# Gate products of an encoder's feed-forward layers by seven quarter-block products, with half of the weight sums made by accumulating DMAs

## The chip, the cores and the metric

The kernel runs on one core of a Trainium2 chip. Its time is device microseconds of one execution, the median of three runs. TensorE (PE in the rows) multiplies, with a second row for its weight loads (PEld); VectorE (DVE), ScalarE (ACT) and GpSimd (POOL) work beside it; SyncE (SP) issues the loads from HBM.

## The reference, cut to what matters

Two layers of an encoder over 512 tokens and width 1024. Each layer is a feed-forward block, a mixer, and a second feed-forward block, so there are four feed-forward blocks (called block 0 to 3 here). Layer 0 mixes by two kinds of attention, layer 1 by convolutions.

```
def swiglu(x, w_gate, w_up, w_down):          # w_gate, w_up: 1024 x 2816
    return (jax.nn.silu(x @ w_gate) * (x @ w_up)) @ w_down
x = x + 0.5 * swiglu(rms_norm(x, ffn_norm[i, 0]), ...)
x = x + mixer(rms_norm(x, mix_norm[i]))
x = x + 0.5 * swiglu(rms_norm(x, ffn_norm[i, 1]), ...)
```

## The kernel before

**Numbers in two parts.** Activations lie as 8 tiles of 128 features x 512 tokens. Each float32 operand is split into a high part (ScalarE's cast, `split`, L146) and a low part (VectorE's subtraction, L147), and each product is three matmuls, high x high, high x low, low x high (`mm3`, L126 to L128).

**A feed-forward block.** The 2816 hidden features are 22 tiles (index f). A tile of `w_gate` or `w_up` is 128 partitions x 1024 columns, 512 KB: eight 128x128 weight blocks, one for each tile of the contraction. A plain product of one tile is 8 x 3 = 24 matmuls of 512 columns (`chunk`). A gate goes through SiLU (`gated`), is multiplied by the up product, and is split again (`hidden`). After 22 tiles the down product follows, 8 output tiles of 22 x 3 matmuls.

**Pairs.** For f = 4 to 19 two hidden tiles are taken together (`pair`). The gate products of the two are plain, 48 matmuls of 512 columns. The up products of both are one product of 2 x 2 blocks (two tiles by two halves of the contraction, times two halves of the contraction by two halves of the tokens) by seven quarter products in place of eight (a Strassen-Winograd scheme): 7 x 4 x 3 = 84 matmuls of 256 columns. Their left factors are sums of weight quarters (`sums`, four VectorE additions of 128x512), their right factors sums of activation quarters (`halves`, made once for each block in four steps, each of some ten small operations on VectorE and ScalarE). The seven results are put together by one ScalarE copy and seven VectorE additions of 128x256. The matmuls of the gates and of the quarter products alternate.

**Weights on their way.** `plan` lists the loads (units) and the splits (pieces of 128x512, each the weights of 12 matmuls); `piece` hands out a piece and sees to it that the next three are loaded, summed and split. Units go through three buffers (`raw`), the two up tiles of a pair through two more (`ux`); high and low pieces have five buffers each. All loads of weights are issued on SP's queue in order (L82), each when its buffer is free. The order of instructions on each engine is fixed when the program is built, by the scheduler of the framework; each engine goes through its list in order.

**Attention.** In the mixer of layer 0, 64 units of attention (32 of one kind, then 32 of the other) run as a pipeline of scores, softmax, transposes (L710) and products with the values. Projections stand between them as fillers: for each unit `mixer_ab` adds 1.6 (first 32 units) or 1.45 (after) blocks of three matmuls.

Of the kernel before, what the change touches and what calls it, by code (L numbers as in the profile page):

```python
# [9 lines left out]
F32 = mybir.dt.float32  # L10
# [13 lines left out]
PAIRS = (4, 20)  # L24
# [4 lines left out]
class Trunk:  # L29
    def __init__(self, ctx, tc, a, out):  # L30
# [8 lines left out]
        self.fr = pool("fr", 1)  # L39
# [19 lines left out]
    def plan(self, units):  # L59


        self.units, self.pieces = [], []
        for u in units:
            i = len(self.units)
            if len(u) == 4:
                g0, g1, u0, u1 = u
                self.units += [(g0, False), (u0, True), (u1, True), (g1, False)]
                A, B = slice(0, 512), slice(512, 1024)
                self.pieces += [(i, A), (i + 1, A), (i + 1, B), (i, B), (i + 2, 0), (i + 2, 1), (i + 3, A), (i + 2, 2), (i + 2, 3), (i + 3, B), (i + 2, B)]
                continue  # L70
            src, cut = u
            self.units.append((src, False))
            w = src.shape[1]
            self.pieces += [(i, slice(c, min(w, c + cut))) for c in range(0, w, cut)]
        self.loaded, self.ready, self.used = [], [], 0
        self.share, self.extra, self.extra_end, self.look = 0, None, 0, 3

    def load(self, upto):
        while len(self.loaded) < min(upto + 1, len(self.units)):
            src, held = self.units[len(self.loaded)]  # L80
            t = (self.ux if held else self.raw).tile([P, 1024], F32, tag="raw", name=self.name("raw"))
            self.nc.sync.dma_start(t[:, : src.shape[1]], src)  # L82
            self.loaded.append(t)

    def sums(self, i):
# [5 lines left out]
        s1, s2, s3, s4 = (self.t() for _ in range(4))  # L91
# [94 lines left out]
    def norm(self, after=None):  # L186

        nc = self.nc
        s = self.fr.tile([P, 2, T], F32R, tag="fr", name=self.name("ss"))
# [28 lines left out]
    def ffn(self, own, gain, natural=False, start=False):  # L218
# [4 lines left out]
        with self.tc.tile_pool(name=self.name("hp"), bufs=NF) as hp, self.tc.tile_pool(name=self.name("ux"), bufs=2) as self.ux, self.tc.tile_pool(name=self.name("tp"), bufs=4) as tp:  # L223
            hs, held = [], []
            if start:
# [13 lines left out]
                xs = list(self.xs)  # L239
            prep = self.halves(hp, tp, own)  # L240
            f = 2 if start else 0
            while f < NF:
                if PAIRS[0] <= f < PAIRS[1]:
                    self.go(prep)
                    hs += self.pair(hp, xs, fold)
# [4 lines left out]
                if f == 0:  # L250
# [8 lines left out]
                    self.norm(AF.Silu)  # L259
                else:  # L260
                    self.go(self.chunk(pg, xs))
                    if held:
                        self.norm(AF.Silu)
# [64 lines left out]
    def pair(self, hp, xs, fold):  # L328

# [3 lines left out]
        gates = [self.ps("g"), self.ps("g")]  # L333
        both = ((j, n) for j, ps in enumerate(gates) for n, _ in enumerate(self.chunk(ps, xs)))
        sn, uu, u0 = self.t(), self.t(), self.t()
        gate = []

        def blocks(n):
            for _ in range(n):
                j, k = next(both)  # L340
                if k == NK - 1:
                    gate.append(self.gated(gates[j], fold))

        def product(tag, x):
            ps = self.ps(tag, 256)
# [10 lines left out]
        blocks(2)  # L356
        q1 = product("g", b11)
        nc.scalar.copy(sn[:, L], q1)
        blocks(2)
        add(u0[:, L], product("d", b21), sn[:, L])  # L360
        blocks(2)
        add(sn[:, R], product("d", part(1)), sn[:, L])
        blocks(2)
        q5 = product("g", part(0))
        add(u0[:, R], q5, sn[:, R])
        blocks(2)
        add(uu[:, L], product("d", part(2)), sn[:, R])
        add(uu[:, R], q5, uu[:, L])
        blocks(2)
        add(u0[:, R], product("d", b22), u0[:, R])  # L370
        blocks(2)
        q4 = product("d", part(3))
        h0 = self.t()
        nc.vector.tensor_tensor(h0, u0, gate[0], op=ALU.mult)
        out = [self.hidden(hp, h0)]
        blocks(2)
        add(uu[:, L], q4, uu[:, L])
        h1 = self.t()
        nc.vector.tensor_tensor(h1, uu, gate[1], op=ALU.mult)
        return out + [self.hidden(hp, h1)]  # L380
# [204 lines left out]
    def put(self, t, p, half):  # L585
# [6 lines left out]
        if half == 1:  # L592
            f = self.t()[:, :n]
            if t % 2 == 0:
                nc.scalar.activation(f, p[:, :n], AF.Copy, scale=r)
            else:
                nc.vector.tensor_scalar(f, p[:, :n], r, 1.0, op0=ALU.mult, op1=ALU.mult)
            p, r = f, None
# [5 lines left out]
        for src, hi, lo in parts:  # L604
            if half == 1:
                nc.gpsimd.tensor_copy(hi, src)
                nc.vector.tensor_tensor(lo, src, hi.bitcast(F32), op=ALU.subtract)
                continue
# [186 lines left out]
    def mixer_ab(self, gain):  # L795
        nc = self.nc
        with ExitStack() as ctx:
            pool = lambda name, bufs: ctx.enter_context(self.tc.tile_pool(name=name, bufs=bufs))
            self.vp, self.up, self.ptp = pool("vp", 4), pool("up", 14), pool("ptp", 4)
# [20 lines left out]
            with self.tc.manual_schedule(engines={mybir.EngineType.PE}):  # L820
# [6 lines left out]
                for i in range(n + 5):  # L827
# [7 lines left out]
                    due += (1.6 if i < 32 else 1.45) / 2  # L835
# [3 lines left out]
                    due += (1.6 if i < 32 else 1.45) / 2  # L839
# [94 lines left out]
    def gated_pair(self, j):  # L934
        nc = self.nc
        pg, pa = self.ps("g"), self.ps("g")
        if j == 0:
# [7 lines left out]
            self.norm(AF.Sigmoid)  # L945
# [147 lines left out]
    def ffn_units(self, i):  # L1093
        a = self.a
        u = []
        for f in range(NF):
# [6 lines left out]
            elif PAIRS[0] <= f < PAIRS[1]:  # L1103
                if f % 2 == 0:
                    u.append((g, a["gate"][i, f + 1], v, a["up"][i, f + 1]))
# [117 lines left out]
```

## Time and profile before

| what | value |
|---|---|
| median of three runs | 1828.51 us (1827.61 to 1831.22) |
| the profiled execution | 1826.34 us, its span 1824.6 us |
| granted TensorE clock, mean | 0.996 |
| busy, share of the span | PE 99%, PEld 85%, DVE 68%, ACT 46%, POOL 10% |
| DMA | 181.79 MB, 31.1% of the 16 engines' time on SP's queue |

A row of a timeline has the start in us, the duration, the engine, the line of the kernel, the operation, its tiles, and in brackets how long the engine had been idle and what it had waited for. Durations of neighbours on one engine overlap, since they are pipelined: what an instruction takes of an engine in a dense stretch is the distance between starts. In the rows `psg`, `psd`, `psm` are the PSUM tiles of the three tags g (four buffers), d (two) and m (two).

### The profile page before, as it was taken

What the parts mean: (1) busy time and instruction counts of PE and PEld (TensorE: products, weight loads), DVE (VectorE), ACT (ScalarE), POOL (GpSimd) and SP (SyncE); (2) the same over time, 40 slices, a digit from 0 to 9 for tenths busy, and PEclk for the clock granted to TensorE, in tenths of its full rate; (3) what the DMA queues carried; (4) which work ended last, traced back from release to release, by engine and by line L of the source; (5) the groups of instructions that cost most, each with busy time, mean ns of one, the idle gap of its engine ahead of it and who ended that gap; (6) DMA issues with size and microseconds to landing.
All of it is one profiled execution on the core that took longest, in us unless ns stands there. A gap on an engine that the chain in (4) does not pass through costs nothing.

```text
span 1824.6 us, 25574 instructions
## 1 busy us (share of the span) xinstructions
PE 1805.4 (99%) x9532; PEld 1555.3 (85%) x9532; DVE 1240.1 (68%) x2211; ACT 842.7 (46%) x1536; POOL 187.2 (10%) x213
## 2 busy tenths in 40 slices
PE   9999999999999999999999999999999999999997
PEld 7899888889878899988888999888888889998886
DVE  6877734488987877764448777634499688887333
ACT  6544433357776544443335444433364554444332
POOL 0000000004432000000000000000389100000000
PEclk9999999999999999999999999999999999999999
DMA  5232233333243232333332332233322232323332
GB/s 198 81 105 93 93 96 95 98 103 99 68 132 114 94 103 96 102 113 96 96 101 81 101 108 93 89 95 96 126 93 93 81 105 94 103 99 96 92 100 66
DMA packets 57675, 181.79 MB, mean 100 GB/s; under 512 B 6352, under 2 KB 8656, under 8 KB 57552
## 3 DMA queue, kind: packets, MB, share of 16 engines
q1 hardware_dynamic: 56976, 179.33, 31.1%
q8 instruction: 75, 1.23, 0.3%
q10 hardware_dynamic: 576, 0.84, 0.1%
q14 instruction: 48, 0.39, 0.1%
HBM read 175.43 MB, written 2.10 MB: 97 GB/s over the span
## 4 chain that ended last, share of the span: by engine, by line
PE 94%; DVE 4%; ACT 1%; DMA 1%; issue 1%; DVEq 0%; SPq 0%; ACTq 0%
PE psg L127 16%; PE psg L126 16%; PE psg L128 16%; PE psd L127 15%; PE psd L128 15%; PE psd L126 15%; PE psm L710 1%; DVE pt L717 1%; DVE wl L147 0%; DMA bias<-in_bias 0%; PE psg L740 0%; PE psg L739 0%; DVE m L673 0%; DVE t L690 0%; PE psg L672 0%
## 5 line engine op out<-in xcount | busy, mean ns | idle before, releaser
L146 ACT CAST wh<-raw 128x512 fp32r<-128x512 f32 (+1 forms) x630 | 380.2, 606 | 616.4 <-PE psd L127 411.9
L147 DVE TENSOR_TENSOR wl<-raw,wh 128x512 fp32r<-128x512 f32 (+1 forms) x556 | 374.5, 674 | 303.3 <-ACT wh L146 297.8
L127 PE MATMUL psg<-xs,wh 128*128 128x512 f32 (+1 forms) x1200 | 455.6, 380 | 0.3 <-DVE xs L156 0.3
L126 PE MATMUL psg<-xs,wh 128*128 128x512 f32 (+1 forms) x1200 | 455.2, 380 | 0.6 <-ACT xs L155 0.6
L128 PE MATMUL psg<-xs,wl 128*128 128x512 f32 (+1 forms) x1200 | 453.2, 378 | 0.0
L128 PE MATMUL psd<-h,wl 128*128 128x512 f32 (+1 forms) x726 | 277.9, 383 | 0.0
L127 PE MATMUL psd<-h,wh 128*128 128x512 f32 (+1 forms) x726 | 277.9, 383 | 0.0
L126 PE MATMUL psd<-h,wh 128*128 128x512 f32 (+1 forms) x726 | 277.7, 383 | 0.0
L128 PEld LDWEIGHTS psg<-xs,wl 128*128 128x128 f32 x1200 | 225.9, 188 | 41.2
L126 PEld LDWEIGHTS psg<-xs,wh 128*128 128x128 f32 x1200 | 226.5, 189 | 37.4 <-ACT xs L155 1.2
L127 PEld LDWEIGHTS psg<-xs,wh 128*128 128x128 f32 x1200 | 226.5, 189 | 36.7 <-DVE xs L156 0.9
L147 POOL TENSOR_TENSOR wl<-raw,wh 128x512 fp32r<-128x512 f32 (+1 forms) x74 | 97.5, 1328 | 766.4 <-ACT wh L146 766.2
L126 PEld LDWEIGHTS psd<-h,wh 128*128 128x128 f32 x726 | 136.4, 188 | 26.8
L128 PEld LDWEIGHTS psd<-h,wl 128*128 128x128 f32 x726 | 136.4, 188 | 26.6
L127 PEld LDWEIGHTS psd<-h,wh 128*128 128x128 f32 x726 | 136.4, 188 | 26.4
L146 ACT CAST wh<-t 128x512 fp32r<-128x512 f32 x128 | 79.4, 621 | 88.2 <-PE psg L127 47.7
L355 DVE TENSOR_TENSOR t<-psd,t 128x256 f32<-128x256 f32 x160 | 67.8, 423 | 71.2 <-PE psd L128 71.2
L126 PE MATMUL psd<-tt,wh 128*128 128x256 f32 x384 | 108.5, 283 | 1.8 <-ACT wh L146 1.8
L128 PE MATMUL psd<-tt,wl 128*128 128x256 f32 x384 | 108.9, 284 | 0.1
L127 PE MATMUL psd<-tt,wh 128*128 128x256 f32 x384 | 108.7, 283 | 0.0
L126 PE MATMUL psd<-xs,wh 128*128 128x256 f32 (+1 forms) x344 | 108.1, 314 | 0.0
L128 PE MATMUL psd<-xs,wl 128*128 128x256 f32 (+1 forms) x344 | 106.9, 311 | 0.0
(275 smaller groups left out, 2702.6 us busy)
## 6 DMA issues: line engine op xcount, KB each, us to landing
raw<-in_up SPq DMA_DIRECT2D x83, 512.0 KB, 3.6
raw<-in_gate SPq DMA_DIRECT2D x83, 512.0 KB, 3.5
raw<-in_down SPq DMA_DIRECT2D x64, 448.0 KB, 3.3
raw<-in_down SPq DMA_DIRECT2D x32, 512.0 KB, 3.5
raw<-in_cdin SPq DMA_DIRECT2D x18, 512.0 KB, 3.5
raw<-in_abqk SPq DMA_DIRECT2D x13, 512.0 KB, 3.5
raw<-in_about SPq DMA_DIRECT2D x16, 256.0 KB, 2.7
bias<-in_bias SPq DMA_DIRECT2D x8, 512.0 KB, 3.5
```

The source lines that it names most:

```text
L126: mm(ps, lhsT=aH, rhs=bH, start=first, stop=False)
L127: mm(ps, lhsT=aH, rhs=bL, start=False, stop=False)
L128: mm(ps, lhsT=aL, rhs=bH, start=False, stop=last)
L146: self.nc.scalar.copy(hi, src)
L147: (eng or self.nc.vector).tensor_tensor(lo, src, hi.bitcast(F32), op=ALU.subtract)
L355: add = lambda to, a, b: nc.vector.tensor_tensor(to, a, b, op=ALU.add)
L710: nc.tensor.transpose(ps[:, i * P : (i + 1) * P], pr[:, i * P : (i + 1) * P], self.ident)
L717: nc.vector.tensor_tensor(lo, src, hi.bitcast(F32), op=ALU.subtract)
```

## The change

**Both products by seven.** In 18 pairs (`BOTH`: four, five, five and four in blocks 0 to 3) the gate products, too, are made by seven quarter products. `pair` now calls a generator `seven` once (other pairs) or twice (these pairs). The pairs named here as double pairs have 168 matmuls of 256 columns and none of 512; the 13 single pairs keep 48 and 84. Block 0 begins its pairs at f = 6, not 4, so there are 31 pairs and not 32, and of its four `halves` steps one now follows each of f = 2 to 5.

**Two of four sums by DMA.** The signs of the scheme are turned so that all four sums of weights are additions. Of these, VectorE makes two (L109, L110). The other two are made while loading: the first quarter of the second tile is loaded twice, into both halves of its buffer (L93, L94), and then GpSimd's queue adds the first tile's quarter into one half (L95) and the second tile's second quarter into the other (L96), by accumulating DMAs of 256 KB that wait for the plain loads. The second quarter by itself goes to a tile of its own (L97, `a22`). A summed unit has thus five DMAs of 256 KB in place of one of 512 KB.

**Smaller edits.** The last projection of the attention's values is scaled and split out of PSUM by ScalarE and VectorE at once (`put`), without the copy and GpSimd's casts. The fillers between units are paced at 1.6 to unit 31, 1.8 to unit 50, 1.35 after. One buffer (`fr`) moves to the mixer's pools.

```
-PAIRS = (4, 20)
+PAIRS = ((6, 20), (4, 20), (4, 20), (4, 20))
+BOTH = ((8, 10, 14, 16), (6, 8, 12, 14, 18), (6, 8, 12, 14, 18), (6, 10, 14, 18))
...
+            if held in (2, 4):
+                A, B = slice(0, 512), slice(512, 1024)
+                a22 = self.a22[len(self.loaded)] = self.ux.tile([P, 512], F32, tag="a22", name=self.name("a22"), bufs=2)
+                self.nc.sync.dma_start(t[:, A], src[:, A])
+                self.nc.sync.dma_start(t[:, B], src[:, A])
+                self.nc.gpsimd.dma_start(t[:, A], self.units[len(self.loaded) - 1][0][:, A], accum_op=ALU.add)
+                self.nc.gpsimd.dma_start(t[:, B], src[:, B], accum_op=ALU.add)
+                self.nc.sync.dma_start(a22, src[:, B])
...
-        nc.vector.tensor_tensor(s1, b[:, A], b[:, B], op=ALU.add)
-        nc.vector.tensor_tensor(s2, a[:, A], s1, op=ALU.subtract)
-        nc.vector.tensor_tensor(s3, b[:, A], a[:, A], op=ALU.subtract)
-        nc.vector.tensor_tensor(s4, a[:, B], s2, op=ALU.add)
-        self.sum4 = s2, s1, s3, s4
+        s2, s4 = self.t(), self.t()
+        nc.vector.tensor_tensor(s2, a[:, A], b[:, B], op=ALU.add)
+        nc.vector.tensor_tensor(s4, a[:, B], s2, op=ALU.add)
+        self.sum4 = s2, b[:, B], b[:, A], s4, self.a22[i]
...
+        if both:
+            for g in self.seven(xs, "gdggdgd", lambda: None):
+                nc.vector.tensor_tensor(g, g, self.rB, op=ALU.mult)
+                nc.scalar.activation(g, g, AF.Silu)
+                if not fold:
+                    nc.vector.tensor_tensor(g, g, self.rB, op=ALU.mult)
+                gate.append(g)
...
-                    next(prep, 0)
+                    if not start:
+                        next(prep, 0)
...
-                    due += (1.6 if i < 32 else 1.45) / 2
+                    due += (1.6 if i < 32 else 1.8 if i < 51 else 1.35) / 2
```

**What moves, in three places.** The first is VectorE in block 0, ahead of the first pair (f = 4): `x`, `par` and `tt` belong to `halves`, `raw` alone to the sums of weights (L92, L93), `wl` to low parts. Before:

```order
L317 TENSOR_TENSOR t_589<-x 128x256
L147 TENSOR_TENSOR tt_410<-t_472,tt_410 128x256
L322 SCALAR_TENSOR_TENSOR t_591<-x,par,t_590 128x256
L323 SCALAR_TENSOR_TENSOR t_530<-x,par,t_528 128x256
L92 TENSOR_TENSOR t_623<-raw_544 128x512
L147 TENSOR_TENSOR tt_525<-t_528,tt_525 128x256
L147 TENSOR_TENSOR tt_412<-t_474,tt_412 128x256
L321 SCALAR_TENSOR_TENSOR t_589<-t_589,par,t_590 128x256
L320 SCALAR_TENSOR_TENSOR tt_524<-t_589,par,tt_524 128x256
L147 TENSOR_TENSOR tt_526<-t_591,tt_526 128x256
L147 TENSOR_TENSOR tt_527<-t_530,tt_527 128x256
```

In the changed program, around the products of f = 4, which are plain now:

```order
L303 TENSOR_TENSOR t_634<-psg_564,rB_378 128x512
L162 TENSOR_TENSOR wl_619<-raw_582,wh_618 128x512
L162 TENSOR_TENSOR tt_452<-t_550,tt_452 128x256
L162 TENSOR_TENSOR wl_666<-raw_582,wh_665 128x512
L311 TENSOR_TENSOR t_638<-psg_565,t_635 128x512
L335 TENSOR_TENSOR t_647<-x 128x256
L162 TENSOR_TENSOR wl_684<-raw_616,wh_683 128x512
L340 SCALAR_TENSOR_TENSOR t_649<-x,par,t_648 128x256
L339 SCALAR_TENSOR_TENSOR t_647<-t_647,par,t_648 128x256
L162 TENSOR_TENSOR h_640<-t_638,h_640 128x512
L338 SCALAR_TENSOR_TENSOR tt_643<-t_647,par,tt_643 128x256
```

Where two steps of `halves` and the sums stood in one stretch, less than one step now stands among the gate (L303, L311) and the low parts of plain products.

The second is VectorE in block 1. Before, around the sums of the pair f = 6 (`h` is a hidden tile, L355 puts quarter products together, L285 takes a gate from PSUM):

```order
L92 TENSOR_TENSOR t_7115<-raw_7045 128x512
L93 TENSOR_TENSOR t_7116<-raw_6934,t_7115 128x512
L94 TENSOR_TENSOR t_7117<-raw_7045,raw_6934 128x512
L147 TENSOR_TENSOR h_7094<-t_7092,h_7094 128x512
L95 TENSOR_TENSOR t_7118<-raw_6934,t_7116 128x512
L147 TENSOR_TENSOR wl_7124<-t_7116,wh_7123 128x512
L147 TENSOR_TENSOR wl_7148<-t_7115,wh_7147 128x512
L355 TENSOR_TENSOR t_7101<-psd_7146,t_7099 128x256
L147 TENSOR_TENSOR wl_7167<-raw_7047,wh_7166 128x512
L147 TENSOR_TENSOR wl_7178<-t_7117,wh_7177 128x512
L285 TENSOR_TENSOR t_7200<-psg_7097,rB_6537 128x512
L147 TENSOR_TENSOR wl_7206<-t_7118,wh_7205 128x512
```

In the changed program, at the passage from the double pair f = 8 to the single pair f = 10. The last low part from the buffer that `raw_7816` takes over (that of `raw_7566`) stands four rows ahead of these; L365 and L366 put quarter products together, L402 multiplies by the gate:

```order
L162 TENSOR_TENSOR wl_7799<-a_1743_7567,wh_7798 128x512
L365 TENSOR_TENSOR t_7740<-psg_7779,t_7740 128x256
L162 TENSOR_TENSOR wl_7824<-raw_7674,wh_7823 128x512
L366 TENSOR_TENSOR t_7741<-t_7740,psg_7797 128x256
L162 TENSOR_TENSOR wl_7845<-raw_7715,wh_7844 128x512
L366 TENSOR_TENSOR t_7742<-t_7740,psd_7815 128x256
L162 TENSOR_TENSOR wl_7867<-raw_7715,wh_7866 128x512
L365 TENSOR_TENSOR t_7741<-psg_7841,t_7741 128x256
L366 TENSOR_TENSOR t_7742<-psg_7797,t_7742 128x256
L162 TENSOR_TENSOR wl_7893<-raw_7674,wh_7892 128x512
L402 TENSOR_TENSOR t_7741<-t_7741,t_7599 128x512
L109 TENSOR_TENSOR t_7905<-raw_7715,raw_7816 128x512
```

Four sums have become two, and evictions of quarter products (`psg`, `psd`, 128x256) stand between the low parts; the sum in the last row is the one that waits for an accumulating DMA (`raw_7816`).

The third is SP's queue in block 1, in the pairs f = 6 to 10. Before, one load for each tile:

```order
L82 DMA raw_7113<-in_gate 128x1024
L82 DMA raw_7045<-in_up 128x1024
L82 DMA raw_7277<-in_gate 128x1024
L82 DMA raw_7164<-in_up 128x1024
L82 DMA raw_7343<-in_gate 128x1024
```

In the changed program:

```order
L99 DMA raw_7674<-in_gate 128x1024
L97 DMA a_1713_7418<-in_gate 128x512
L99 DMA raw_7523<-in_up 128x1024
L93 DMA raw_7566<-in_up 128x512
L94 DMA raw_7566<-in_up 128x512
L97 DMA a_1743_7567<-in_up 128x512
L99 DMA raw_7842<-in_gate 128x1024
L99 DMA raw_7903<-in_gate 128x1024
L97 DMA a_1794_7817<-in_up 128x512
L99 DMA raw_7715<-in_up 128x1024
L93 DMA raw_7816<-in_up 128x512
```

A summed tile (`raw_7566`, `raw_7816`) has become two loads of half its size and a third for its own quarter (`a_1743_7567` is `a22`). The accumulating DMAs onto it stand on GpSimd's queue.

## Rows read from the trace of the kernel before

**Rows 1.** Engines on the page: busy time, share of the span, instructions.
```profile
PE 1805.4 (99%) x9532; PEld 1555.3 (85%) x9532; DVE 1240.1 (68%) x2211; ACT 842.7 (46%) x1536; POOL 187.2 (10%) x213
```
**Rows 2.** The chain that ended last, by engine: share of the span.
```profile
PE 94%; DVE 4%; ACT 1%; DMA 1%; issue 1%; DVEq 0%; SPq 0%; ACTq 0%
```
**Rows 3.** Windows: two pairs, then down product; length, busy (instructions), PEclk, DMA share, GB/s.
```profile
684.81:726.97 42.16, 42.16 (x266) 38.10 (x265) 32.68 (x57) 18.81 (x34) 0.00 (x0) 1.00 0.30 100
...
1200.00:1300.00 100.00, 100.00 (x443) 82.84 (x442) 41.51 (x65) 31.40 (x54) 0.00 (x0) 1.00 0.32 93
```
**Rows 4.** Timeline of ScalarE: the copy of one pair and of the pair two later.
```profile
684.81 0.37 ACT L358 COPY t<-psg 128x256 f32<-128x256 f32 x1
...
726.97 0.36 ACT L358 COPY t<-psg 128x256 f32<-128x256 f32 x1
```
**Rows 5.** Timeline of TensorE: first and last of 20 quarter matmuls, and the next.
```profile
668.81 0.28 PE L128 MATMUL psd<-tt,wl 128*128 128x256 f32 x1
...
671.08 0.28 PE L128 MATMUL psg<-tt,wl 128*128 128x256 f32 x1
671.20 0.40 PE L128 MATMUL psg<-xs,wl 128*128 128x512 f32 x1
```
**Rows 6.** Timeline of VectorE in a pair, back to back, then a sum that needs the one before.
```profile
685.32 0.68 DVE L95 TENSOR_TENSOR t<-raw,t 128x512 f32<-128x512 f32 x1
685.92 1.29 DVE L147 TENSOR_TENSOR wl<-t,wh 128x512 fp32r<-128x512 f32 x2
687.12 0.42 DVE L355 TENSOR_TENSOR t<-psd,t 128x256 f32<-128x256 f32 x1
687.46 0.68 DVE L147 TENSOR_TENSOR wl<-raw,wh 128x512 fp32r<-128x512 f32 x1
...
703.86 0.69 DVE L92 TENSOR_TENSOR t<-raw 128x512 f32<-128x512 f32 x1
704.58 0.69 DVE L93 TENSOR_TENSOR t<-raw,t 128x512 f32<-128x512 f32 x1
```
**Rows 7.** Lines by form, VectorE, those two pairs: busy, mean ns, idle before, releaser.
```profile
L147 DVE TENSOR_TENSOR wl<-raw,wh 128x512 fp32r<-128x512 f32 x14 | 9.6, 688 | 1.6 <-ACT wh L146 1.3
...
L355 DVE TENSOR_TENSOR t<-psd,t 128x256 f32<-128x256 f32 x10 | 4.2, 424 | 4.6 <-PE psd L128 4.6
```
**Rows 8.** Windows around the first pair of block 0, columns as in rows 3.
```profile
55.00:59.00 4.00, 4.00 (x25) 3.44 (x23) 4.00 (x11) 2.51 (x6) 0.00 (x0) 1.00 0.00 0
59.00:62.50 3.50, 1.38 (x7) 0.70 (x5) 3.50 (x9) 2.19 (x6) 0.00 (x0) 1.00 0.00 0
62.50:66.20 3.70, 3.59 (x15) 2.87 (x16) 3.70 (x8) 2.11 (x5) 0.00 (x0) 0.54 0.41 142
```
**Rows 9.** Timeline of TensorE there: the stall, and seventeen matmuls later.
```profile
58.89 0.39 PE L128 MATMUL psg<-xs,wl 128*128 128x512 f32 x1
61.09 0.39 PE L126 MATMUL psd<-tt,wh 128*128 128x256 f32 x1 [1.81 <-ACT wh L146]
...
65.83 0.40 PE L126 MATMUL psd<-tt,wh 128*128 128x256 f32 x1
```
**Rows 10.** Timeline of TensorE in the second kind of attention: two stalls.
```profile
542.06 0.28 PE L688 MATMUL psg<-bk,bq 128*128 128x256 f32 x1
543.69 0.52 PE L710 MATMUL psm<-ident,pb 128*128 128x128 f32 x3 [1.34 <-DVE rz L698]
...
544.92 0.28 PE L688 MATMUL psg<-bk,bq 128*128 128x256 f32 x1
546.69 0.41 PE L710 MATMUL psm<-ident,t 128*128 128x128 f32 x2 [1.49 <-DVE pt L717]
```
**Rows 11.** Waits of TensorE, 440 to 575 us: total, times, longest.
```profile
PE psm L710 <- DVE pt L717: 2.7, 3, 1.5
PE psm L710 <- DVE rz L698: 1.5, 2, 1.3
```
**Rows 12.** DMA issues: line, queue, count, KB each, median us from issue to landing.
```profile
raw<-in_up SPq DMA_DIRECT2D x83, 512.0 KB, 3.6
...
raw<-in_about SPq DMA_DIRECT2D x16, 256.0 KB, 2.7
...
x<-in_x SPq DMA_DIRECT2D x8, 256.0 KB, 4.7
```
**Rows 13.** Timeline of SP's queue: one issue.
```profile
671.51 0.33 SPq L82 DMA_DIRECT2D raw<-in_gate  x1
```

More of the change, by code (lines that the diff above doesn't have):

```diff
@@ L184, in root, with norm @@
         nc.vector.scalar_tensor_tensor(y, a, 1.5, e, op0=ALU.add, op1=ALU.mult)
-    def norm(self, after=None):
+    def norm(self, after=None, pool=None):
         nc = self.nc
-        s = self.fr.tile([P, 2, T], F32R, tag="fr", name=self.name("ss"))
+        pool, tag = pool or (self.fr, "fr")
+        s = pool.tile([P, 2, T], F32R, tag=tag, name=self.name("ss"))
         self.split(s[:, 0], s[:, 1], self.S)
@@ L239, in ffn @@
                 xs = list(self.xs)
+            p0, p1 = PAIRS[own // 8]
             prep = self.halves(hp, tp, own)
@@ L242, in ffn @@
             while f < NF:
-                if PAIRS[0] <= f < PAIRS[1]:
+                if p0 <= f < p1:
                     self.go(prep)
-                    hs += self.pair(hp, xs, fold)
+                    hs += self.pair(hp, xs, fold, f in BOTH[own // 8])
                     f += 2
@@ L326, in halves, with seven, product @@
             yield
-    def pair(self, hp, xs, fold):
+    def seven(self, xs, tags, between):
         nc = self.nc
         L, R = slice(0, 256), slice(256, 512)
[L333 to L345, printed above, removed]
+        sn, u0, u1 = self.t(), self.t(), self.t()
+        tags = iter(tags)
+        def product(x):
+            between()
+            ps = self.ps(next(tags), 256)
             h, l = self.piece()
@@ L355, in pair @@
         add = lambda to, a, b: nc.vector.tensor_tensor(to, a, b, op=ALU.add)
[L356 to L380, printed above, removed]
+        sub = lambda to, a, b: nc.vector.tensor_tensor(to, a, b, op=ALU.subtract)
@@ new lines, in seven, with pair, between, join @@
+        nc.scalar.copy(sn[:, L], product(b11))
+        add(u0[:, L], product(b21), sn[:, L])
+        add(sn[:, R], product(part(1)), sn[:, L])
+        q5 = product(part(0))
+        sub(u0[:, R], sn[:, R], q5)
+        sub(u1[:, L], sn[:, R], product(part(2)))
+        sub(u1[:, R], q5, u1[:, L])
+        add(u0[:, R], product(b22), u0[:, R])
+        yield u0
+        sub(u1[:, L], product(part(3)), u1[:, L])
+        yield u1
+    def pair(self, hp, xs, fold, both):
+        nc = self.nc
+        gate, out = [], []
+        if both:
+            for g in self.seven(xs, "gdggdgd", lambda: None):
[4 more added lines that the diff above has]
+                gate.append(g)
+            between = lambda: None
+        else:
+            gates = [self.ps("g"), self.ps("g")]
+            blocks = ((j, n) for j, ps in enumerate(gates) for n, _ in enumerate(self.chunk(ps, xs)))
+            def between():
+                for _ in range(2):
+                    j, k = next(blocks)
+                    if k == NK - 1:
+                        gate.append(self.gated(gates[j], fold))
+        def join(u):
+            nc.vector.tensor_tensor(u, u, gate[len(out)], op=ALU.mult)
+            out.append(self.hidden(hp, u))
+        ups = self.seven(xs, "gdggdgd" if both else "gddgddd", between)
+        first = next(ups)
+        if both:
+            join(first)
+            join(next(ups))
+        else:
+            last = next(ups)
+            join(first)
+            between()
+            join(last)
+        return out
```

48 lines of the change are left out of this document (21 added, 27 removed).

## The prediction

> **What bounds the kernel now.** The page's engine list comes first: TensorE is busy for 99% of the span, VectorE for 68%, ScalarE for 46% [rows 1], and the chain that ended last runs through TensorE for 94% of the span [rows 2]. So time is won where TensorE gets less to do or where it waits, and other engines count only where they make it wait. Second, the windows: in a stretch of two pairs TensorE is busy throughout at a granted clock of 1.00, VectorE for 32.68 of 42.16 us, DMA for 30% [rows 3]. Nothing is idle on TensorE there, so what a pair costs is its matmuls, and VectorE has the least room beside it. Third, timelines for the distances between starts: a pair takes 21.08 us (42.16 over two) [rows 4], a matmul of 256 columns 0.1195 us (2.39 over 20) [rows 5], a wide one in the down product 0.226 us (100 over 443) [rows 3]. On VectorE a 128x512 operation takes 0.60 us in a dense stretch and 128x256 takes 0.34; 0.72 where a sum needs the one just before [rows 6]. Last, two places where TensorE does wait: the first pair of block 0 [rows 8, 9] and the second kind of attention [rows 10, 11].
>
> **The change part by part.**
>
> *Fewer matmul columns.* A double pair has 168 quarter matmuls: 168 x 0.1195 = 20.08 us against 21.08, so 1.00 us less, 18.0 us in 18 pairs. That is the most it can give. The pair f = 4 of block 0 goes back to plain products: 96 x 0.226 = 21.7 us, 0.6 more.
>
> *What VectorE has to do beside it.* In a double pair it makes 14 low parts, 4 sums, 2 gate scalings, 2 gate-by-up products and 2 low parts of hidden tiles, 24 operations of 128x512, and 14 evictions of 128x256. Dense, that is 24 x 0.60 + 14 x 0.34 = 19.2 us, under TensorE's 20.08; in block 3, where the gate is scaled a second time, 26 operations and 20.4 us, over it. Each by its own duration (688 and 424 ns [rows 7]) it would be 22.4 us. The pairs of now show where between these it falls: the window's 43 wide and 14 narrow operations are 30.6 us dense and take 32.68, 7% more [rows 3], since evictions wait for TensorE (4.6 us in those two pairs [rows 7]). With 7% on top a double pair is 20.5 us, in block 3 21.8. Three pieces lie ready ahead of TensorE, and a single pair (19 wide and 7 narrow operations, 13.8 us of 21.08) stands between every one or two double ones, so some of the lag is caught up, and I take 20.4 us, and 21.0 in block 3. That leaves 0.7 x 14 + 0.1 x 4 = 10.2 us of the 18.0. ScalarE, with 14 casts more than half empty, hides the silu and copies.
>
> The Trainium skill ("TensorE: Matmul & The Clock Gate", Back-to-back issue gap) gives a warm matmul N / 2.4 + 2.5 ns, 109 ns for 256 columns and 216 for 512. By that a double pair would save 48 x 0.216 - 84 x 0.109 = 1.2 us, 21.8 in all; the rows are about 11 ns above it at either width, and the sum goes by the rows.
>
> *The accumulating DMAs.* Two sums leave VectorE for 98 accumulating DMAs (two for each summed tile). No row shows one. They cost nothing while they land before the sum that VectorE still makes, which in-order VectorE waits for with evictions and low parts queued behind it. The tightest place is the passage from a double to a single pair, nine times: the buffer of the second up tile comes free 15 VectorE rows before the sum that needs it again, 8 wide and 6 narrow between, 6.8 us dense. After the sum about 3 us remain until TensorE wants its product (one quarter product, three more with 18 gate matmuls between them, 8.4 us, less some 5 us of VectorE's work before and after the sum). So about 10 us are there. The chain needs two issues (0.66 us [rows 13]), the plain loads (2.7 us [rows 12]) and two accumulations. From below one is a plain 256 KB load, 2.7 us; from above the slowest 256 KB load of the trace, 4.7 us [rows 12]. I take the 512 KB load, 3.6 us, since an accumulation reads both operands. One behind the other at SP's spacing the chain ends at 7.3 us; in strict series at 10.6 (6.1 and 12.8 with the bounds). I take no cost. In other places a buffer is free a whole unit earlier. SP's loads behind these wait a little longer, and DMA's share rises from 0.30 by the bytes of a double pair (3.5 MB instead of 2 MB) and the second operand, to some 0.6.
>
> *The first pair of block 0.* TensorE waits there from 58.89 to 61.09 us and then crawls: 17 matmuls until 65.83 us, 3 wide and 14 narrow, worth 2.36 us, take 6.94 [rows 9]. VectorE is busy without a gap while TensorE has 1.38 us of work in 3.5, and the clock granted after that is 0.54 on the mean, part of it at the lower level of 1.2 GHz [rows 8]. The cause is that two steps of `halves` and the sums stand in one stretch of VectorE ahead of the first product that needs them. In the changed order the steps lie among four plain tiles, and the first `tt` comes two tiles later. I take all 4.6 us as gone (at worst none).
>
> *Attention.* Two stalls of 1.51 and 1.65 us beyond the usual 0.12 [rows 10] stand where no filler is between scores and transposes; before them 18 blocks ran in a row. At 1.8 and 1.35 the fillers are spread. Waits for transposes are 4.2 us in all [rows 11]. I take 2.5 us as gone, between 4.2 and, if stalls move to another unit, -2. `put` trades casts of GpSimd for small operations of ScalarE, under fillers on TensorE, at nothing; without this cover about 1 us.
>
> *Sum.* -10.2 + 0.6 - 4.6 - 2.5 = -16.7 us. The profiled execution took 1826.34 us, so 1809.6 by itself; it is 2.2 under the median of 1828.51, which becomes 1812.
>
> **The rivals.**
>
> *VectorE becomes the bound.* Double pairs take 21 us or more (7% above dense, and dependent sums at 0.72), so the 18.0 is lost whole: 1828.5 + 0.6 - 4.6 - 2.5 = 1822 us, up to 1827 with longer double pairs. For it: 96% of TensorE's time, with in-order evictions. Against it: single pairs between, and the dense stretch of rows 6.
>
> *TensorE gets it all.* VectorE keeps to 20.08 us in blocks 0 to 3 and every wait for transposes goes: -18.0 + 0.6 - 4.6 - 4.2, 1802 us.
>
> *The accumulated sum comes late* (slower). If the two accumulations together take more than 6.6 us (10 less 0.66 and 2.7), the sum blocks VectorE and TensorE runs dry at each of the nine passages. Rows 9 show what a stall of 2 us costs, with the slower clock behind it: 4.6 us. Nine of them are 41 us: 1853 us. For it: the strict series of 10.6 us. Against it: loads on SP's queue follow each other at 0.33 us.
>
> The Trainium skill ("SBUF — State Buffer", SBUF: two separate sides) warns that GpSimd cannot write the descriptors of its DMAs while VectorE holds their shared port in a two-port mode, as a float32 copy does. No run here shows such a DMA yet. By its wording the additions and subtractions of a pair don't hold that port; if VectorE's dense stretches held it all the same, the accumulations would wait for the 0.8 us that VectorE is idle in a double pair, and the time is that of the late sum, 1853 or more. I give that 0.03, inside the 0.15 of the late sum.
>
> **How the numbers follow.** Forecast 0.56 (its own range 1805 to 1819), VectorE the bound 0.17, all of it 0.12, late sum 0.15. Range 1800 to 1830: the low end is just under the second rival, the high end includes the first, and most of the late sum is left out. This kernel's measurement can tell 0.2% from no change, 3.7 us. Faster than 1824.8 are the forecast, the second rival and 0.13 of the first, 0.81; within 0.2% 0.04 of the first and 0.02 of a mildly late sum, 0.06; slower the rest, 0.13.
>
> **What would show it.** Starts of the first quarter product in successive double pairs: 20.1 to 20.6 us in blocks 0 to 2 and about 21 in block 3; at 21 everywhere VectorE is the bound, and its idle time there is near nothing. A wait of L109 for a DMA of GpSimd's queue, with TensorE idle after it and a lower granted clock, shows the late sum. In block 0 the clock stays at 1.00 to the end of the pairs. In the attention the waits of L710 fall from 4.2 us to under 2. I am wrong if an accumulation lands more than 5 us after its issue, or if double pairs are no shorter than single ones.

## The result, and the profile after

The changed kernel takes 1802.99 us (median of four runs, 1801.81 to 1803.78) against 1828.06 of the kernel before beside it: a ratio of 0.986 with the interval 0.984 to 0.988, 25 us less. The sign, the range and most of the places were as predicted; the gain is half again as large as the forecast's 16.7 us, and 1803 us lies below the forecast's own range of 1805 to 1819. The page of the changed kernel, its engines and its chain, answers to [rows 1, 2]:

```profile
PE 1786.6 (99%) x10144; PEld 1571.7 (87%) x10144; DVE 1268.6 (70%) x2349; ACT 874.6 (49%) x1610; POOL 268.1 (15%) x303
...
PE 97%; DVE 1%; DMA 1%; ACT 0%; issue 0%; POOL 0%; SPq 0%; DVEq 0%; ACTq 0%; POOLq 0%
```

TensorE is the bound as before, with more matmuls in less time, and its share of the chain has grown from 94% to 97%. Where the 23.9 us of the span went is read from the starts of the first and last down matmul of each block, which stand in both timelines (here the first of block 0, before and then in the changed kernel):

```profile
245.79 0.39 PE L126 MATMUL psd<-h,wh 128*128 128x512 f32 x1
```
```profile
238.67 0.39 PE L141 MATMUL psd<-h,wh 128*128 128x512 f32 x1
```

| stage | before | changed | difference |
|---|---|---|---|
| to block 0's down product | 245.79 | 238.67 | -7.12 |
| attention, and block 1 to its down product | 463.57 | 455.27 | -8.30 |
| block 2 to its down product | 234.62 | 230.12 | -4.50 |
| convolutions, and block 3 to its down product | 389.24 | 385.81 | -3.43 |
| four down products | 480.08 | 480.07 | -0.01 |
| end | 11.30 | 10.76 | -0.54 |

The stages of blocks 2 and 3 lose about 0.9 us for each double pair in them (5 and 4); those of block 0 and of the attention lose 3 to 4 us beyond that.

**A double pair.** ScalarE's copy of the first quarter product marks the gate half and the up half of a double pair, and then the next double pair (timeline, answers to [rows 4]); the window is from the first of these rows to the third, columns as in [rows 3]:

```profile
650.70 0.36 ACT L367 COPY t<-psg 128x256 f32<-128x256 f32 x1
660.74 0.37 ACT L367 COPY t<-psg 128x256 f32<-128x256 f32 x1
670.82 0.37 ACT L367 COPY t<-psg 128x256 f32<-128x256 f32 x1
```
```profile
650.70:670.82 20.12, 20.12 (x170) 20.12 (x169) 18.83 (x37) 10.69 (x20) 1.77 (x2) 1.00 0.68 167
```

A double pair takes 20.12 us, TensorE is busy throughout, and VectorE for 18.83 us. The forecast had laid 1.3 us on top of VectorE's dense work, and so past TensorE's time; here VectorE is idle for 1.3 us inside it.

**The accumulating DMAs.** From the page (answers to [rows 12]), then the passage from the double pair f = 8 to the single pair f = 10 in block 1: the plain loads on SP's queue, the two accumulations on GpSimd's, and VectorE at the sum.

```profile
raw<-in_up SPq DMA_DIRECT2D x72, 256.0 KB, 3.4
raw<-in_up POOLq DMA_DIRECT2D x62, 256.0 KB, 5.5
...
raw<-in_gate POOLq DMA_DIRECT2D x36, 256.0 KB, 6.1
```
```profile
681.70 0.33 SPq L93 DMA_DIRECT2D raw<-in_up  x1
682.08 0.77 SPq L94 DMA_DIRECT2D raw<-in_up  x1
...
685.00 0.86 POOL L95 DMA_DIRECT2D raw<-in_up  x1 [19.00 <-DVE t L365]
686.18 0.89 POOL L96 DMA_DIRECT2D raw<-in_up  x1 [0.32 <-issue]
...
688.92 0.68 DVE L402 TENSOR_TENSOR t<-t,t 128x512 f32<-128x512 f32 x1
691.50 0.69 DVE L109 TENSOR_TENSOR t<-raw,raw 128x512 f32<-128x512 f32 x1 [1.89 <-DMA raw<-in_up]
```

From the first load's issue to the sum are 9.8 us: 3.3 us of plain loads, 1.2 us between the two issues on GpSimd, and 5.3 us until the second accumulation is there. VectorE, in order, stands idle for 1.89 us. Over the run (view of the sum's line):

```profile
its engine sat idle before it (us, times) until:
  DMA raw<-in_up: 15.2, 9
```

Nine times, once at each passage: the wait that the third rival needed is there, 1.1 to 2.5 us and 1.7 on the mean, but TensorE has no stall in any pair.

**The two stalls.** Windows of block 0's first pairs, and of the attention where the two stalls of [rows 10] were; then the waits of TensorE from 425 to 560 us, answering to [rows 11]:

```profile
58.00:66.20 8.20, 8.20 (x38) 6.80 (x37) 5.08 (x12) 4.24 (x10) 0.00 (x0) 1.00 0.29 99
540.00:548.00 8.00, 8.00 (x50) 6.97 (x49) 6.65 (x24) 5.95 (x18) 2.46 (x6) 1.00 0.51 151
```
```profile
PE psd L141 <- DVE v L634: 1.1, 2, 0.8
PE psg L711 <- DMA bk<-bk: 0.6, 1, 0.6
PE psm L734 <- DVE pt L741: 0.3, 1, 0.3
```

TensorE is busy throughout at a granted clock of 1.00, and its waits for transposes (L734 now) fell from 4.2 to 0.3 us. The new `put` adds 1.1 us of waits for the values that it writes (`v`, L634). One gain was not forecast. Ahead of the first unit of attention the granted clock of the kernel before falls (first row); the changed kernel, 7 us ahead in its program there, keeps 1.00 (second row):

```profile
402.00:412.00 10.00, 10.00 (x73) 9.91 (x73) 8.38 (x23) 4.37 (x7) 0.00 (x0) 0.83 0.28 81
```
```profile
396.00:404.00 8.00, 8.00 (x70) 7.91 (x69) 7.32 (x21) 3.96 (x7) 0.00 (x0) 1.00 0.23 70
```

0.83 over 10 us is 1.7 us of lost work. Just before it fell, TensorE ran 32 matmuls of two columns (first row); the changed kernel runs the same 32 (second row) and keeps its clock:

```profile
402.90 3.63 PE L541 MATMUL psm<-sel,sq 128*128 128x2 f32 x32
```
```profile
395.86 3.63 PE L576 MATMUL psm<-sel,sq 128*128 128x2 f32 x32
```

From block 0's down product to the first scores of the attention the two kernels give TensorE the same 315 matmuls in the same order. So TensorE's own work there does not tell the two apart; what does stays open.

### The profile page after: what moved, and what is told of

It reads as the page before. It is cut to its first block, busy times and chain, and to the rows that moved or that the text cites. A ratio compares the mean times of both kernels' runs of the same rounds, so it can differ in the third digit from the quotient of the medians.

```text
span 1800.7 us, 27637 instructions
## 1 busy us (share of the span) xinstructions
PE 1786.6 (99%) x10144; PEld 1571.7 (87%) x10144; DVE 1268.6 (70%) x2349; ACT 874.6 (49%) x1610; POOL 268.1 (15%) x303
## 3 DMA queue, kind: packets, MB, share of 16 engines
q8 instruction: 80, 1.31, 0.3%
## 4 chain that ended last, share of the span: by engine, by line
PE 97%; DVE 1%; DMA 1%; ACT 0%; issue 0%; POOL 0%; SPq 0%; DVEq 0%; ACTq 0%; POOLq 0%
PE psd L143 16%; PE psd L142 16%; PE psd L141 16%; PE psg L141 15%; PE psg L142 15%; PE psg L143 15%; PE psm L734 1%; PE psg L764 1%; PE psg L763 1%; DMA bk<-bk 0%; DMA x<-in_x 0%; PE psg L695 0%; PE psg L696 0%; PE psm L576 0%; PE psg L711 0%
## 5 line engine op out<-in xcount | busy, mean ns | idle before, releaser
L161 ACT CAST wh<-raw 128x512 fp32r<-128x512 f32 (+1 forms) x662 | 400.1, 607 | 580.4 <-PE psd L142 325.7
L162 DVE TENSOR_TENSOR wl<-raw,wh 128x512 fp32r<-128x512 f32 (+1 forms) x588 | 393.9, 673 | 290.8 <-ACT wh L161 284.5
L142 PE MATMUL psg<-xs,wh 128*128 128x512 f32 (+1 forms) x1140 | 408.7, 359 | 0.3 <-DVE xs L171 0.3
L141 PE MATMUL psg<-xs,wh 128*128 128x512 f32 (+1 forms) x1140 | 407.5, 359 | 0.6 <-ACT xs L170 0.6
L143 PE MATMUL psg<-xs,wl 128*128 128x512 f32 (+1 forms) x1140 | 406.6, 358 | 0.0
L143 PEld LDWEIGHTS psg<-xs,wl 128*128 128x128 f32 x1140 | 215.2, 189 | 31.8
L141 PEld LDWEIGHTS psg<-xs,wh 128*128 128x128 f32 x1140 | 215.7, 189 | 30.4 <-ACT xs L170 1.4
L142 PEld LDWEIGHTS psg<-xs,wh 128*128 128x128 f32 x1140 | 215.8, 189 | 29.2 <-DVE xs L171 0.9
L142 PE MATMUL psd<-tt,wh 128*128 128x256 f32 x444 | 125.6, 283 | 0.0
L143 PE MATMUL psd<-tt,wl 128*128 128x256 f32 x444 | 125.6, 283 | 0.0
L141 PE MATMUL psd<-tt,wh 128*128 128x256 f32 x444 | 125.4, 282 | 0.0
L161 ACT CAST wh<-t 128x512 fp32r<-128x512 f32 x98 | 60.6, 619 | 127.2 <-DVE t L109 66.9
L141 PE MATMUL psd<-xs,wh 128*128 128x256 f32 (+1 forms) x336 | 106.7, 318 | 0.0
L142 PE MATMUL psd<-xs,wh 128*128 128x256 f32 (+1 forms) x336 | 104.6, 311 | 0.0
```

The source lines that it names most:

```text
L141: mm(ps, lhsT=aH, rhs=bH, start=first, stop=False)
L142: mm(ps, lhsT=aH, rhs=bL, start=False, stop=False)
L143: mm(ps, lhsT=aL, rhs=bH, start=False, stop=last)
L161: self.nc.scalar.copy(hi, src)
L162: (eng or self.nc.vector).tensor_tensor(lo, src, hi.bitcast(F32), op=ALU.subtract)
```

## The experiments

Two theories stood against each other on the main term. A: TensorE's matmuls set the pace of a double pair; VectorE costs time only by dense work above TensorE's. B, the forecast's: VectorE needs 7% more than its dense work, and part of the 18 us is lost to its lag.

**What the double pairs are worth** (`single_gates`).
```
-BOTH = ((8, 10, 14, 16), (6, 8, 12, 14, 18), (6, 8, 12, 14, 18), (6, 10, 14, 18))
+BOTH = ((), (), (), ())
```


> The changed kernel with all 31 pairs single (the gate products of the 18 double pairs are plain again); accumulating DMAs, block 0's order and attention as changed. Theory A (TensorE's matmuls set the pace of a double pair, VectorE's waits for quarter products are slack, and nothing else limits it): the 18 pairs take back 0.9 us each, the difference of the stage times of blocks 1 and 2, 16.2 us in all: 1819 us, and the stages of blocks 0 to 3 up to their down products grow by 3.6, 4.5, 4.5 and 3.6 us. Theory B (the forecast's: VectorE's lag eats part of each, only 10.2 us were gained, the rest came from elsewhere): 1813 us.

Measured 1820.33 us, 17.3 more than the changed kernel. The stages with blocks 0, 2 and 3 grew by 3.7, 4.6 and 3.7 us, 0.93 us a pair, 16.7 us in 18. The fourth grew by 5.8 us, 1.1 more than its five pairs, since the granted clock falls at 403 us as in the kernel before. A holds, B falls.

**All pairs double** (`all_double`).
```
-BOTH = ((8, 10, 14, 16), (6, 8, 12, 14, 18), (6, 8, 12, 14, 18), (6, 10, 14, 18))
+BOTH = (range(0, 22), range(0, 22), range(0, 22), range(0, 22))
```


> The changed kernel with all 31 pairs double, so that no single pair stands between for VectorE to catch up. Theory A (dense VectorE work of 19.2 us fits 20.1 us; 20.4 us in block 3 lags by 0.3 us a pair, 2.6 us over eight, within the ready pieces): 13 more pairs by 0.9 us, 1791 us. Theory B (7% above dense, 20.5 and 21.8 us): TensorE waits 0.4 us in 23 pairs and 1.7 us in eight, 1814 us. Theory C (the accumulated sums come late at every passage between two double pairs, where a buffer is free only just before): stalls of TensorE in most pairs, above 1815 us, with L109 waiting for GpSimd's queue more than ten times.

Measured 1791.95 us (1790.19 to 1792.02), ratio to the kernel before 0.980 (0.978 to 0.981): 11 us faster than the changed kernel, as A has it, and the fastest of all. Windows of this kernel in block 1 and in the last pairs of block 3, and copies there:

```profile
640.00:740.00 100.00, 100.00 (x836) 100.00 (x835) 95.24 (x188) 54.13 (x98) 17.59 (x20) 1.00 0.74 179
...
1584.00:1620.00 36.00, 36.00 (x302) 36.00 (x301) 36.00 (x72) 20.54 (x40) 5.27 (x6) 1.00 0.73 181
```
```profile
1574.88 0.37 ACT L367 COPY t<-psg 128x256 f32<-128x256 f32 x1
1584.95 0.37 ACT L367 COPY t<-psg 128x256 f32<-128x256 f32 x1
1595.05 0.37 ACT L367 COPY t<-psg 128x256 f32<-128x256 f32 x1
1605.20 0.36 ACT L367 COPY t<-psg 128x256 f32<-128x256 f32 x1
1615.35 0.36 ACT L367 COPY t<-psg 128x256 f32<-128x256 f32 x1
```

In block 1 VectorE is 95% busy and costs nothing. At the end of block 3 it has no idle time. Through the sixth pair there a half still takes 10.08 us (first two rows), as in the other blocks; in the last two pairs it takes 10.15, so a double pair is 20.30 us, beside the 20.4 of dense work in the prediction. There, and only there, VectorE is the bound. Theory C fell: the sum waits 6.8 us in 3 times.

**What the two sums by DMA are worth** (`sums_on_vector`, and `all_double_sums_on_vector` with every pair double).
```
-                self.nc.sync.dma_start(t[:, A], src[:, A])
-                ...
-                self.nc.gpsimd.dma_start(t[:, B], src[:, B], accum_op=ALU.add)
+            self.nc.sync.dma_start(t[:, : src.shape[1]], src)
...
+        nc.vector.tensor_tensor(s1, b[:, A], b[:, B], op=ALU.add)
+        nc.vector.tensor_tensor(s2, a[:, A], s1, op=ALU.add)
+        nc.vector.tensor_tensor(s3, b[:, A], a[:, A], op=ALU.add)
```


> The changed kernel with all four sums of weights on VectorE again and every weight tile loaded plainly, double pairs kept. A double pair then has 28 wide and 14 narrow VectorE operations, 21.6 us dense (22.8 in block 3) against 20.1 of TensorE. Theory A (only dense work above TensorE's time counts, and three ready pieces of 1.43 us and the next single pair take up a lag of 1.5 to 3 us): no stall of TensorE, or a few us in all, 1803 to 1808 us. Theory B (VectorE needs 7% more than dense): 23.1 and 24.4 us, lags of 3 to 6 us in each run of double pairs, beyond the 4.3 us that lie ready: 1820 us or more, with the second half of double pairs longer than 10.1 us.

> All 31 pairs double, with all four sums of weights on VectorE and plain loads. A double pair then asks 28 wide and 14 narrow operations of VectorE, 21.6 us dense (two wide ones more in block 3, 22.8), against 20.16 of TensorE, and no single pair stands between. Theory A (VectorE costs time only by its dense work): once the ready pieces are used up, VectorE is the bound and a double pair takes 21.6 us in blocks 0 to 2 and 22.8 in block 3; 1.44 x 23 + 2.6 x 8 = 54 us less some 4.3 us of ready pieces in each of four blocks: about 1829 us, that is, no gain over the kernel before. Theory B (7% more than dense): periods of 23.1 and 24.4 us, 1875 us. Theory E (the pairs take VectorE's lag in some other way, since the sums need not be dense): under 1810 us.

The first took 1809.09 us, 6.1 more, just above A's 1803 to 1808 and far from B. In its trace TensorE loses some 0.73 us at the end of each of the six runs of two double pairs in a row, 4.4 us in all, and none after a double pair by itself. Its span is 7.0 us longer; the rest is 1.7 us at the kernel's start and 1.1 in the stage of the attention, in both of which the granted clock falls where the changed kernel's does not. The second took 1839.12 us, ratio 1.006 (1.004 to 1.007): slower than the kernel before. Windows of two double pairs of the second, in block 1 and in block 3:

```profile
700.81:743.80 42.99, 42.00 (x339) 40.75 (x338) 42.99 (x86) 21.05 (x41) 0.00 (x0) 1.00 0.32 99
1594.04:1639.43 45.39, 43.42 (x338) 40.98 (x336) 45.39 (x90) 21.06 (x41) 0.00 (x0) 1.00 0.31 94
```

VectorE is busy to the last hundredth, and a double pair takes 21.50 and 22.70 us: the dense sums are 28 x 0.60 + 14 x 0.34 = 21.6, and 22.8 with two more. So the dense rate of [rows 6] is the capacity of VectorE, without 7%. The whole is 10 us above A's 1829: from `all_double` by these periods, 1791.95 + 23 x 1.34 + 8 x 2.54 is 1843 us (against 20.16 us, two halves of 10.08), so of the 17 us of lag that A let the ready pieces absorb only some 4 were. Without the DMA sums, making the other pairs double loses 30 us; with them it gains 11.

**How late a sum may come** (`third_accumulation`).
```
                 self.nc.gpsimd.dma_start(t[:, B], src[:, B], accum_op=ALU.add)
+                self.nc.gpsimd.dma_start(t[:, B], src[:, B], accum_op=ALU.add)
```


> The changed kernel with the second accumulating DMA of every summed tile issued twice, so that the sum lands one accumulation later (that half of the tile then holds the addend twice). Theory A' (the nine waits of VectorE of 1.7 us at the passages from double to single pairs use up most of the slack): with some 5 us more, L109 waits 7 us there, longer than the 4.3 us of ready pieces, TensorE stalls 2 to 4 us at nine passages, some at the lower clock: 1820 to 1845 us. Theory D (the sum has slack far beyond it, or the two run side by side on the queue): 1803 us, L109's waits under 30 us in all.

Measured 1825.53 us (1820.87 to 1834.10 in ten runs), 22.5 more: A' holds. VectorE and then TensorE in block 1, at the passages from f = 8 to 10 and from 14 to 16:

```profile
703.84 0.69 DVE L110 TENSOR_TENSOR t<-raw,raw 128x512 f32<-128x512 f32 x1 [4.51 <-DMA raw<-in_up]
...
769.88 0.69 DVE L110 TENSOR_TENSOR t<-raw,raw 128x512 f32<-128x512 f32 x1 [5.93 <-DMA raw<-in_up]
```
```profile
704.66 0.39 PE L142 MATMUL psg<-xs,wh 128*128 128x512 f32 x1
705.32 0.38 PE L142 MATMUL psd<-tt,wh 128*128 128x256 f32 x1 [0.27 <-ACT wh L162]
...
768.36 0.39 PE L142 MATMUL psg<-xs,wh 128*128 128x512 f32 x1
771.35 0.38 PE L142 MATMUL psd<-tt,wh 128*128 128x256 f32 x1 [2.60 <-ACT wh L162]
```

VectorE waits 4.51 and 5.93 us; TensorE loses 0.4 and 2.8 of them (the distances between starts less 0.23 for the matmul). So VectorE may wait 3.2 to 4.1 us there for nothing. Over the run it waits 4.4 to 5.9 us at each of the nine passages, less than the 7 that were expected, and TensorE loses 10.5 us at them, from nothing to 2.8. In this trace, 20.5 us longer, 5.1 us more go to three falls of the granted clock, one of them the one ahead of the attention. In the changed kernel it waits 1.89 and, at the second passage, 1.31:

```profile
752.36 0.69 DVE L109 TENSOR_TENSOR t<-raw,raw 128x512 f32<-128x512 f32 x1 [1.31 <-DMA raw<-in_up]
```

About 2 us are left. The late sum is a real rival, missed by that much.

**Block 0 and the attention, one at a time.** `block0_order` is the kernel before with pairs from f = 6 in block 0 and one step of `halves` per tile; `pacing_alone` and `put_alone` are the kernel before with the new pace, and with the new `put`; `block0_and_pacing` has the first two; `changed_with_old_pace` and `changed_with_old_put` take one each out of the changed kernel.
```
-PAIRS = (4, 20)
+PAIRS = ((6, 20), (4, 20), (4, 20), (4, 20))
...
-                    due += (1.6 if i < 32 else 1.45) / 2
+                    due += (1.6 if i < 32 else 1.8 if i < 51 else 1.35) / 2
```


> The kernel before with only block 0 changed: its pairs begin at f = 6, and one step of halves follows each of f = 2 to 5. Theory of the prediction: the stall at 59 us and the lower clock after it go, 4.6 us, a plain pair costs 0.6 more: the first down matmul at 241.8 us in place of 245.8, the time 1824 us. Rival (the steps move the stall to f = 6, or the sums alone make it): first down matmul at 246 us, no change or slower by 0.6.

> The kernel before with only the fillers' pace in the attention changed to 1.6, 1.8 and 1.35. Theory of the prediction: the stalls at 542 and 545 us go, 2.5 us: 1825.5 us. Rival (the gain of 3.8 us seen between the blocks comes from the other edit of the attention, put): 1828 us, stalls of the same sum at other units.

> The kernel before with only put changed: the last projection of the values is scaled and split out of PSUM by ScalarE and VectorE at once, without GpSimd. Theory of the prediction: nothing, 1828 us, since fillers cover it. Rival: it takes away waits for the values of the second attention, 1 to 4 us less between 445 and 530 us.

> The kernel before with block 0's order and the fillers' pace of the attention both changed (alone, the first shortened block 0 by 4.0 us but the attention behind it grew by 3.7 with a lower clock after the stalls at 538 us; the second gave 3.3 us). Theory A (the two stalls of the attention stand so that the clock falls in some programs and not in others; the pace removes them, and then block 0's gain stays): 1820.5 us, granted clock 1.00 from 412 us to the end. Rival (moving the attention in time loses block 0's gain whatever the pace): 1824.5 us.

> The changed kernel with the attention's old pace of 1.45 after unit 31. Theory A (the pace removes the two stalls at 542 us and with them the fall of the clock that some programs show there): the stage from block 0's down product to that of block 1 grows from 455.3 us by 2 to 4 us, the stalls of 1.5 us are back behind unit 50, 1805 to 1807 us. Rival (the double pairs or put already moved them away): 1803 us.

> The changed kernel with the old put (a scaled copy out of PSUM, then casts by GpSimd). Theory of the prediction (nothing, covered by fillers): 1803 us, that stage within 0.5 us of 455.3. Rival (put is worth some 1.5 us, the part of the attention's gain that the pace alone did not give on the kernel before): 1804.5 us, with TensorE waiting again for the values between 430 and 530 us.

| kernel | us | beside it | difference |
|---|---|---|---|
| block0_order | 1827.25 | 1827.87 (before) | -0.6, within the scatter |
| pacing_alone | 1824.51 | 1827.87 (before) | -3.4 |
| put_alone | 1827.28 | 1827.87 (before) | -0.6, within the scatter |
| block0_and_pacing | 1823.10 | 1827.79 (before) | -4.7 |
| changed_with_old_pace | 1808.76 | 1802.99 (changed) | +5.8 |
| changed_with_old_put | 1803.86 | 1802.99 (changed) | +0.9, within the scatter |

The first is a miss in the whole and a hit at its place. Its first down matmul starts at 241.78 us, the 4.0 us that were expected:

```profile
241.78 0.39 PE L126 MATMUL psd<-h,wh 128*128 128x512 f32 x1
```

but the attention behind it took 3.7 us more. Windows of 540 to 550 us, of `block0_order` and then of `pacing_alone`:

```profile
540.00:550.00 10.00, 7.81 (x34) 6.74 (x35) 7.63 (x27) 6.47 (x20) 2.85 (x6) 0.66 0.47 131
```
```profile
540.00:550.00 10.00, 8.88 (x54) 7.23 (x54) 9.13 (x29) 7.53 (x21) 3.96 (x7) 1.00 0.59 158
```

In the kernel before such stalls left the clock alone; here the granted clock is 0.66 behind them, for part of the window the lower level of 1.2 GHz. With the pace changed TensorE is busier there and keeps 1.00. The stall of block 0, too, is followed by a fall in one program and not in another: in `put_alone`, where block 0 is that of the kernel before, TensorE has the same 1.38 us of work in 3.5, and then a granted clock of 1.00 in place of the 0.54 of [rows 8]:

```profile
59.00:62.50 3.50, 1.38 (x6) 0.79 (x6) 3.50 (x8) 2.19 (x6) 0.00 (x0) 1.00 0.00 0
62.50:66.20 3.70, 3.31 (x24) 2.84 (x24) 3.70 (x8) 2.25 (x5) 0.00 (x0) 1.00 0.43 142
```

Its first down matmul starts 1.1 us earlier than in the kernel before, so about that much of the 4.0 us hangs on a fall that the same stall need not bring.

Put back into the changed kernel, the old pace brings 2.6 us of waits for transposes and a lower clock back (0.94 over 520 to 545 us):

```profile
520.00:545.00 25.00, 21.37 (x117) 18.55 (x116) 19.19 (x58) 17.82 (x49) 9.07 (x15) 0.94 0.43 132
```

The stage of the attention grew by 7.5 us in this trace, not the 2 to 4 expected. Of these, 3.4 are the clock at another place, among the 315 matmuls ahead of the first scores, which the pace does not change:

```profile
396.00:406.00 10.00, 10.00 (x59) 9.86 (x60) 7.04 (x21) 3.92 (x7) 0.00 (x0) 0.66 0.18 50
```

So the pace is worth 3.4 us alone; of the 5.8 us in the changed kernel some 3 are not its own. With both edits the gain is 4.7 us, between the theory and its rival; in its trace, the fastest of seven runs, block 0 is 3.4 us and the attention 2.0 us shorter, and the clock stays at 1.00 after 407 us, as the theory had it. `put` is worth nothing that these runs can tell: the waits for `v` are gone with the old one, and 2.2 us of waits for transposes stand in their place. The move of `fr` was not tried by itself.

**Pairs from f = 2** (`all_double_from_f2`, against `all_double`).
```
-PAIRS = ((6, 20), (4, 20), (4, 20), (4, 20))
+PAIRS = ((6, 20), (2, 20), (2, 20), (2, 20))
```


> All pairs double, and in blocks 1 to 3 the pairs begin at f = 2, not 4: three more pairs in place of plain tiles. Theory A (TensorE's work sets the time): 96 x 0.226 - 20.16 = 1.5 us less in each of three blocks, 1787.5 us. Rival (the steps of halves then stand in one stretch of VectorE ahead of the first pair, as in block 0 of the kernel before, and TensorE runs dry for 2 us with the lower clock after it, 4.6 us a block): 1801 us.

Measured 1813.78 us, 22 more than `all_double`: the rival, and worse. Window of the first pair of block 1:

```profile
609.00:629.00 20.00, 15.44 (x95) 13.09 (x94) 19.97 (x47) 11.12 (x26) 1.77 (x2) 0.91 0.42 96
```

VectorE is busy throughout and TensorE for 15.44 us of 20: the steps of `halves`, the sums and the gates of plain tiles stand in one stretch. It is the stall of [rows 8] again, and blocks 2 and 3 have it too:

```profile
961.00:981.00 20.00, 16.78 (x120) 14.80 (x118) 19.96 (x46) 11.55 (x26) 1.76 (x2) 1.00 0.46 112
1465.00:1485.00 20.00, 15.57 (x99) 14.14 (x98) 19.89 (x46) 11.85 (x29) 1.76 (x2) 0.83 0.37 93
```

The clock falls behind two of the three. Not all of the 22 us are theirs: another 3.4 us are a fall of the clock ahead of the attention.

## Why the prediction was right, and where its size was off

*Fewer columns.* 1.00 us a pair was predicted as the most; 0.93 to 0.96 was measured (20.12 against 21.08). Right. The formula from the Trainium skill ("TensorE: Matmul & The Clock Gate", Back-to-back issue gap) is the page's for a matmul by itself, not for a stream, which the prediction does not say; the sum went by the rows, and they held.

*VectorE beside it: the mis-sized term.* The step "With 7% on top a double pair is 20.5 us, in block 3 21.8", and from it 10.2 us of the 18.0, measured 16.7. The step put the 7% down to VectorE's waits for TensorE, but they stood in its busy time, 32.68 us, which holds no waits. An operation of 128x512 with a wait behind it is counted with its whole 0.69 us, and one that is followed at once with the 0.60 us to the next start [rows 6]; the 24 waits of over 0.05 us in the window, at 0.09 us each, make up the difference of 2.1 us. It goes as the waits go: in 640 to 740 us of `all_double` VectorE's busy 95.24 us are 118 wide and 69 narrow operations, 94.3 us dense. So neither the waits nor the 7% are a rate; they are room. Only dense work above TensorE's time costs, which the periods of 21.50 and 22.70 us show. In block 3 of the changed kernel, where dense work is 20.4 us, a single pair or plain tiles follow each double one, and no stall of TensorE shows. These 6.5 us are most of the gap between forecast and result.

*The accumulating DMAs.* Right in that they cost nothing, wrong in both sizes that led there. They land 5.5 and 6.1 us after their issue, above the bound of 4.7 us, and by its own test ("more than 5 us after its issue") that step failed. The chain took 9.8 us, inside 6.1 to 12.8, where 7.3 was taken. And the budget was not 10 us but some 12: 9.8 and the 2 us that are left. By the prediction's own budget 0.2 us would have been left in place of 2.7; the rest of what is left comes from the budget's error, and that is luck. The bound from above failed since the nearest rows were plain loads.

Of the rule that VectorE can keep GpSimd from writing its DMAs' descriptors (the Trainium skill, "SBUF — State Buffer", SBUF: two separate sides) no run here shows a sign: in `all_double`, VectorE has no idle time from 1560 to 1620 us (first row), and the six accumulations for gate tiles issued there landed 6.6 us after their issue (second row), the median of the whole run too.

```profile
1560.00:1620.00 60.00, 60.00 (x502) 60.00 (x501) 60.00 (x120) 31.60 (x61) 9.82 (x12) 1.00 0.74 180
```
```profile
raw<-in_gate POOLq DMA_DIRECT2D x6, 256.0 KB, 6.6
```

VectorE's operations here are additions, subtractions and products of float32; the copies that the page names were not tried.

*Block 0.* -4.6 and +0.6 were predicted, -4.0 measured by itself at its place, though its whole kernel gained nothing clear of the scatter. Right in mechanism; of the size, `put_alone` gains 1.1 us without the edit, where the clock does not fall.

*Attention.* -2.5 predicted, some 3.6 found by the stages (8.3 less five pairs at 0.93). Waits for transposes fell to 0.3 us, under the 2 us that were named. But 1.7 us of the 3.6 are the fall of the clock near 405 us, which was not forecast. It comes and goes between kernels that run the same matmuls there (gone in `all_double` and `changed_with_old_put`, there in `single_gates`), and what decides it stays open. Without it 1.9 us are left, under the 2.5: the total of this term is right by luck in part.

*The sum.* 16.7 of the pairs, 4.0 of block 0 and 3.6 of the attention are 24.3 us; measured were 23.9 in the span and 25.1 in the medians. That is the time of the rival "TensorE gets it all", 1802 us, which had a chance of 0.12. The range held because it took in this rival; the forecast's own term did not lead there.

## What to carry to other kernels

For an engine beside the bound, count its dense work against the bound's time and nothing else; its waits for the bounding engine are room, until a window shows it busy to the last hundredth. Then a gain that stops short is looked for in what still stands between the good stretches: here the single pairs, 11 us. An edit that frees time ahead of a fragile place is measured at its own stage, since the whole can lose it again behind, as block 0's 4.0 us in the attention.

## What the runs showed of the hardware

In the changed kernel an accumulating DMA of 256 KB lands 5.5 to 6.1 us after issue (medians), where a plain one of the same size takes 3.4 to 3.5, and its issue keeps GpSimd for 0.9 to 1.2 us where most of SP's take 0.33. For its bytes it also takes the DMA engines twice the time (page of the changed kernel: SP's queue, then GpSimd's; MB and share of the 16 engines):

```profile
q1 hardware_dynamic: 71088, 192.18, 34.5%
...
q0 software_dynamic: 14112, 25.70, 9.0%
```

Much the same stalls in the same stage of the attention left the granted clock at 1.00 in the kernel before (5.06 us of TensorE in 540 to 548 us) and at 0.66 in `block0_order`; the same stall in the same block left it at 0.54 in the kernel before and at 1.00 in `put_alone`; and the same 315 matmuls ran with and without a fall. So the clock's share of a stall's price is not read from one trace.
